# First layer of a hybrid encoder trunk: where the scalar columns, the gate's low-rank product and the squares of the second half stand in the order of work

## Chip, core and metric

One core of a Trainium2 chip runs the whole program. The metric is the device time of one execution in microseconds; the time shown is a median over several runs. The engines are called as the profile does: PE (matrix products), PEld (loading of their stationary operand), DVE (VectorE), ACT (ScalarE), POOL (GpSimd), SP (SyncE, which here issues the loads).

## What is computed

The reference is a two-layer encoder on a sequence of 1024 tokens with 1024 channels, all in float32. The first layer (even) feeds two groups of heads from one input projection of the normalised input; the second (odd) is attention over chunks. Each has a squared-ReLU MLP and a gated embedding behind it. The change touches the first layer only, of which this matters:

```python
h = rmsnorm(x, norm_mix_g[i])
proj = h @ even_w_in[e]
dh = token_shift(h) - h
# group A, RWKV-7
xw = h + dh * mu_lora[0]
xa = h + dh * mu_lora[1]
xg = h + dh * mu_lora[2]
w_log = -jax.nn.softplus(-(w0 + jnp.tanh(xw @ w1) @ w2).astype(jnp.float32)) - 0.5
a = jax.nn.sigmoid(a0 + (xa @ a1) @ a2)
g = jax.nn.sigmoid(xg @ g1) @ g2
...
y = y.reshape(bsz, seq, A_WIDTH) * g.astype(jnp.float32)
# group B, gated DeltaNet
beta = jax.nn.sigmoid(beta_logit.astype(jnp.float32))
g = -jnp.exp(a_log.astype(jnp.float32)) * jax.nn.softplus((alpha_logit + dt_bias).astype(jnp.float32))
...
gc = jnp.cumsum(g, -1)
```

`g` of group A is the gate; its low-rank products are `xg @ g1` and then `@ g2`. `beta_logit` and `alpha_logit` are eight columns of `proj`, the scalar columns; `gc` is their cumulated decay. `rmsnorm` needs the sum of squares of each token over all channels.

## The kernel before

The first layer works on the transposed input, 128 channels on the partitions and tokens along the free axis. The sequence is cut in two halves of 512 tokens (`HB`), and the heads in 4 pairs of group A ("rwkv") and 4 heads of group B ("gdn"). That makes 16 units, in the order half, pair, group (`units`, line 533): units 0, 2, 4, 6 are rwkv and 1, 3, 5, 7 gdn of the first half, 8 to 15 the same of the second.

Six lanes, written as generators, are woven together by `run` (line 135), which keeps a clock of its own and takes the first lane that is due: post, back, mid and front of a unit, the cumulated decays (`gdn_cums`), and last `l0_in`, which projects the inputs of every unit. `l0_in` is so the filler: its products are written down where no other lane is due. The tile framework then puts the instructions of each engine in an order of its own, by priority and by an estimate of when each can run, so an instruction that depends on nothing can stand far ahead of its place in the program.

`l0_in` (line 560) does this for each half. At its first unit (0 or 8) it loads the eight channel blocks of `x`, scales them into pairs of a rounded and a remainder part (`xg`), and forms the low-rank product of decay and learning rate (`lora(0, ...)`, result `lwa`). It projects the unit's inputs (`rwkv_in`, three matrices; `gdn_in`, four with the gate), each a dense product of 24 matmuls (`project`, `dense_part`). At line 644, behind the inputs of units 0 and 8, follow the scalar columns (`gdn_scalars`, line 716: 16 matmuls with the tile `wba`, an eviction to `ba`, four transposes, then some thirty operations on 16 columns, most on DVE, to `gs_beta` and `gs_g`) and the gate's low-rank product (`lora(1, ...)`, result `lgo`). Later units' inputs wait for buffers of units before them: unit u's input j needs `("raw", u - 2, j)`, and a gdn unit's gate `("front", u - 2)`.

What waits for the two: `gdn_cums` for `("g", hf)`, and then each gdn unit's front for `("gc", hf)` (line 1063); each rwkv unit's post for `("lg", hf)` (line 1050).

`lora` (line 691) loads one matrix (`lraw`), makes two scaled copies of it on POOL (line 704), and splits each into a rounded part (`whi`, ACT, line 298) and a remainder (`wlo`, DVE, line 299) before its two dense products. Loaded weights, `lraw`, its scaled copies, the raw columns of `wba`, `ba` and the second product's result `sb` are all tiles of one ring, `wraw`, of two buffers; `whi` and `wlo` have two each.

Squares for the normalisation: for the first half they are taken of the tiles just loaded. For the second half, line 632 loads `x` once more, four times two blocks through the ring `pl` of the pool `pre`, behind unit 6's inputs; `square` (line 666) squares on ACT and adds on POOL into `acc`. Unit 7 turns that into row statistics (line 641), used from unit 8 on. Unit 8 loads the second half's `x` again for `xg`, one pair through `pl` and three through `wraw` (line 574).

Of the kernel before, what the change touches and what calls it, by code (L numbers as in the profile page):

```python
# [8 lines left out]
F32 = mybir.dt.float32  # L9
# [8 lines left out]
P = 128  # L18
# [3 lines left out]
HB = 512  # L22
# [93 lines left out]
class Trunk:  # L116
# [443 lines left out]
    def l0_in(self, units):  # L560
        nc, a, fr = self.nc, self.a, self.fr
        self.state = {}
        self.xg = []
        for u, (nm, p, hf) in enumerate(units):
            if u % 8 == 0:


                self.xg, squares = [], []
                if hf == 0:
                    acc = fr.tile([P, HB], F32, tag="rsbc", name="acc", bufs=2)  # L570
                    self.w_first = self.load_w(a["w_in"][4])
                else:

                    x2 = [self.load_x(q, self.pre if q == 1 else self.wp, "pl" if q == 1 else "wraw")
                          for q in range(4)]
                for k in range(NK):
                    if hf == 0:
                        xr = self.t2()
                        nc.sync.dma_start(out=xr, in_=a["x"][k, :, 0:HB])
                    else:  # L580
                        xr = x2[k // 2][:, k % 2, :]
                    if k % 2 == 0:
                        xg2 = self.pair(k // 2)
                    xg = xg2[:, k % 2]
                    self.split_scaled(xg, xr, self.vec("mixg", k), slice(0, HB))
                    self.xg.append(xg)
                    if hf == 0:
                        squares.append(lambda k=k, xr=xr: self.square(acc, xr, k == 0))
                for f in squares:
                    f()  # L590
                if hf == 0:
                    raw = self.pre.tile([P, 2, 512], F32, tag="ph", name="wa2r")
                    for j in range(2):
                        for r in range(2):
                            nc.sync.dma_start(out=raw[64 * r:64 * r + 64, j], in_=a["wa2"][64 * j:64 * j + 64])
                    hi = self.pre.tile([P, 2, 512], F32R, tag="pl", name="wa2h")
                    nc.scalar.copy(hi, raw)
                    nc.vector.tensor_tensor(raw.bitcast(F32R), raw, hi.bitcast(F32), op=ALU.subtract)
                    self.wa2 = self.dr.tile([P, 2, 2, 512], F32, tag="wa2", name="wa2")
                    nc.sync.dma_start(out=self.wa2[:, 0], in_=hi.bitcast(F32))  # L600
                    nc.sync.dma_start(out=self.wa2[:, 1], in_=raw)
                    self.g2 = self.l0.tile([P, 512], F32, tag="g2", name="g2")
                    nc.sync.dma_start(out=self.g2, in_=a["g2"])
                    self.hv = self.l0.tile([P, 2, 4], F32, tag="hv", name="hv")
                    nc.sync.dma_start(out=self.hv.rearrange("p a b -> p (a b)"),
                                      in_=a["gdnhv"].rearrange("(o c) -> o c", o=1).broadcast_to((P, 8)))
                    self.ea = self.l0.tile([P, 1, 4], F32, tag="ea", name="ea")
                    nc.scalar.activation(self.ea, self.hv[:, 0:1, :], AF.Exp)
                sc = {}
                if hf == 0:  # L610
                    rsc = self.rsc = self.sm.tile([P, 4], F32, tag="rsc", name="rsc")
                    self.rs = fr.tile([P, HB], F32, tag="rsbc", name="rsbc", bufs=2)

                    self.extra = [lambda t=t: self.psm.tile([P, HB], F32, tag=t, name="dps") for t in ("y", "ch", "pm")]
                    self.late, self.plan = [], {2: lambda: self.row_stats([acc], rsc), 3: lambda: self.to_rows(rsc, self.rs)}
                    raws = yield from getattr(self, nm + "_in")(p, hf, u)
                else:
                    self.rs = acc
                self.pst = None
                sc["lwa"] = yield from self.lora(0, [(0, 64, 0), (64, 128, 1)], "la")  # L620
                lwa = sc["lwa"]
                nc.scalar.activation(lwa[0:64], lwa[0:64], AF.Tanh)
                sc["lwa"] = self.pre.tile([P, 2, HB], F32R, tag="ph", name="lwa")
                for j, (r, o) in enumerate(((slice(0, 64), slice(64, 128)), (slice(64, 128), slice(0, 64)))):
                    m = sc["lwa"][:, j]
                    nc.scalar.copy(m[r], lwa[r])
                    nc.vector.tensor_tensor(m[o], lwa[r], m[r].bitcast(F32), op=ALU.subtract)
            if u:
                raws = yield from getattr(self, nm + "_in")(p, hf, u)
            self.state[u] = (raws, sc)  # L630
            self.mark(("in", u), 1.0)
            if u == 6:

                acc = fr.tile([P, HB], F32, tag="rsbc", name="acc", bufs=2)
                for q in range(4):
                    x2 = self.load_x(q, self.pre, "pl")
                    for e in range(2):
                        self.square(acc, x2[:, e], q + e == 0)
            if u == 7:
                rsc = self.rsc = self.sm.tile([P, 4], F32, tag="rsc", name="rsc")  # L640
                self.row_stats([acc], rsc)
                yield "l0_in1"
                self.to_rows(rsc, acc)
            if u % 8 == 0:

                yield from self.gdn_scalars(hf, sc)
                gg = yield from self.lora(1, [(0, 128, 2)], "lg")
                nc.scalar.activation(gg, gg, AF.Tanh, scale=0.5)
                nc.vector.tensor_scalar(gg, gg, 0.5, 0.5, op0=ALU.mult, op1=ALU.add)
                sc["lg"] = gg  # L650
                self.mark(("lg", hf))

        rsb = lambda: fr.tile([P, HB], F32, tag="rsbc", name="xs", bufs=2)
        pt = [self.pair(k) for k in range(2)]
        sc = [self.pair(q, F32) for q in (2, 3)]
        sc = [t[:, e] for t in sc for e in range(2)]
        yield from self.ple_proj(0, lambda k, hf: pt[k][:, hf], sc[0], lambda n: sc[1 + n % 3], rsb, self.load_w)
        yield from self.out_early(0, a["x"], self.pair, rsb, self.load_w, [("post", 7), ("post", 13), ("post", 14), ("post", 15)])

    def load_x(self, q, pool, tag):  # L660

        x2 = pool.tile([P, 2, HB], F32, tag=tag, name="xr")
        self.nc.sync.dma_start(out=x2, in_=self.a["x"][2 * q:2 * q + 2, :, HB:T].rearrange("k p t -> p k t"))
        return x2

    def square(self, acc, x, first):

        nc = self.nc
        sq = acc if first else x
        nc.scalar.activation(sq, x, AF.Square)  # L670
        if not first:
            nc.gpsimd.tensor_tensor(acc, acc, sq, op=ALU.add)
# [123 lines left out]
    def rwkv_in(self, p, hf, u):  # L796
        raws = []
        for j in (1, 0, 2):
            if u >= 2:
                yield ("raw", u - 2, j)  # L800
            w = self.load_w(self.a["w_in"][4 * j + p]) if u or j != 1 else self.w_first
            raws.append((yield from self.project(w, f"r{p}{j}", 1)))
        return [raws[1], raws[0], raws[2]]

    def gdn_in(self, n, hf, u):
        raws = []
        for j in (1, 0, 2):
            if u >= 2:
                yield ("raw", u - 2, j)
            raws.append((yield from self.project(self.load_w(self.a["w_in"][12 + 4 * j + n]), f"g{n}{j}", 3)))  # L810
        if u >= 2:
            yield ("front", u - 2)
        gate = yield from self.project(self.load_w(self.a["w_in"][24 + n]), None, 0, "gate")
        return [raws[1], raws[0], raws[2], gate]
# [414 lines left out]
    def tail(self, i, xsrc):  # L1229
# [13 lines left out]
        with ExitStack() as es:  # L1243
# [153 lines left out]
            def end(*keys):  # L1397
                for key in keys:
                    split_end(*begun.pop(key))
            load_x(0)  # L1400
            load_x(1)
            wn = {2: self.w_next} if i == 0 else {}

# [820 lines left out]
```

## Time and profile before

| | us |
|---|---|
| median of 3 runs | 3088.87 |
| lowest and highest | 3086.13, 3096.15 |
| the profiled execution | 3095.25 |
| its span, first to last instruction | 3093.5 |

In the profiled execution DVE is busy for 72% of the span, ACT for 46% and POOL for 41%; the mean granted clock of PE is 0.969 of full speed. The first layer's sixteen units take about the first quarter of the span. Tables by stage give, for a stretch of the span, its length, then busy time and number of instructions of PE, PEld, DVE, ACT and POOL, the granted clock of PE, the share of time in which the DMA engines worked and what they moved in GB/s. Lines of a timeline give start and duration in us, engine, line of the kernel, operation, output and inputs, shapes and count; in brackets stands how long the engine was idle before and what ended that. Groups of instructions give minimum, median and maximum in ns and the first and last start in us. `SPq` is the queue of SyncE.

### The profile page before, as it was taken

To read this page: it belongs to the slowest core of one execution; us is meant where nothing else is said; L and a number is where in the kernel's file an instruction comes from. 1 tells how busy PE (TensorE), PEld (TensorE's weight loads), DVE (VectorE), ACT (ScalarE), POOL (GpSimd) and SP (SyncE) were. 2 spreads that over 40 slices of the span, in tenths; PEclk is the share of its full clock that TensorE was granted. 3 is DMA by queue.
4 is the path that set the end of the run, shared out by engine and by line. 5 is a ranking of instruction groups with operands and counts; after the bars stand their busy time and mean duration, and the time that the engine had idled before them with its cause. 6 is when DMAs were issued, how large, how long until landed. Compare 5 with 4: busy or idle time off the path is not lost. (4 is left out here: it accounts for less than half of the span.)

```text
span 3093.5 us, 45263 instructions
## 1 busy us (share of the span) xinstructions
PE 2970.1 (96%) x16888; PEld 2493.6 (81%) x16888; DVE 2220.7 (72%) x3680; ACT 1411.6 (46%) x2546; POOL 1256.6 (41%) x1396
## 2 busy tenths in 40 slices
PE   7999899999998999999999899999999999999999
PEld 5787778888786888788888899989887888788887
DVE  6556665666847888877686587877867888877672
ACT  4344443444435444443343465655645444543331
POOL 6244343433613666646354200000113666645442
PEclk8999898999898999999999999999999999999999
DMA  4222112222445333564423211110275433654322
GB/s 134 97 72 65 47 44 76 69 76 78 147 155 197 123 147 149 205 246 164 137 87 124 81 44 37 41 57 20 72 263 208 149 147 147 220 215 173 127 96 102
DMA packets 166765, 374.31 MB, mean 121 GB/s; under 512 B 41360, under 2 KB 45584, under 8 KB 165136
## 3 DMA queue, kind: packets, MB, share of 16 engines
q1 hardware_dynamic: 134288, 312.68, 29.4%
q10 hardware_dynamic: 32256, 58.73, 5.0%
q8 instruction: 133, 2.18, 0.3%
q14 instruction: 88, 0.72, 0.1%
HBM read 259.15 MB, written 112.20 MB: 120 GB/s over the span
## 5 line engine op out<-in xcount | busy, mean ns | idle before, releaser
L173 PE MATMUL dps<-r,act 128*128 128x512 f32 x4440 | 1044.0, 394 | 10.8 <-DVE act L113 9.0
L173 PEld LDWEIGHTS dps<-r,act 128*128 128x128 f32 x4440 | 835.4, 189 | 202.9 <-DVE act L113 17.0
L173 PE MATMUL dps<-xg,whi 128*128 128x512 f32 x1248 | 427.6, 419 | 22.3 <-ACT xg L342 6.7
L113 ACT CAST act<-late 128x512 fp32r<-128x512 f32 (+1 forms) x282 | 205.5, 731 | 443.6 <-DVE late L113 261.2
L113 DVE TENSOR_TENSOR act<-late,act 128x512 fp32r<-128x512 f32 (+1 forms) x282 | 331.8, 1178 | 72.2 <-ACT act L113 68.9
L173 PE MATMUL dps<-wq,act 128*128 128x384 f32 x1536 | 304.5, 346 | 7.2 <-DVE vs L1982 2.5
L173 PEld LDWEIGHTS dps<-xg,whi 128*128 128x128 f32 x1248 | 240.4, 198 | 73.7 <-ACT xg L342 6.7
L173 PEld LDWEIGHTS dps<-wq,act 128*128 128x128 f32 x1536 | 266.1, 191 | 12.2 <-DVE vs L1982 4.1
L173 PE MATMUL dps<-xg,wlo 128*128 128x512 f32 x624 | 257.8, 414 | 1.5 <-DVE wlo L299 1.5
L113 POOL TENSOR_TENSOR late<-late 128x512 f32<-128x512 f32 (+1 forms) x104 | 189.6, 1832 | 76.3 <-ACT late L113 57.9
L113 POOL TENSOR_TENSOR late<-late,rs 128x512 f32<-128x512 f32 x88 | 136.7, 1566 | 103.3 <-DVE late L113 95.3
L1989 POOL TENSOR_TENSOR sq<-qk 128x512 f32<-128x512 f32 x32 | 35.8, 1117 | 315.3 <-ACT qk L1977 289.7
L113 DVE TENSOR_TENSOR r<-act,r 128x1024 fp32r<-128x1024 f32 (+1 forms) x80 | 141.4, 1770 | 6.7 <-ACT r L113 6.7
L173 PEld LDWEIGHTS dps<-xg,wlo 128*128 128x128 f32 x624 | 122.4, 196 | 27.4 <-DVE wlo L299 2.2
L113 DVE TENSOR_TENSOR late<-late 128x512 f32<-128x512 f32 x120 | 142.3, 1186 | 1.0
L173 PE MATMUL dps<-xw,act 128*128 128x512 f32 x576 | 139.2, 394 | 3.7 <-ACT act L113 3.7
L173 PEld LDWEIGHTS dps<-xw,act 128*128 128x128 f32 x576 | 108.7, 189 | 28.5 <-ACT act L113 4.2
L2077 ACT ACTIVATE pb<-pb,mx 128x640 f32<-128x640 f32 (+4 forms) x128 | 89.5, 699 | 86.7 <-DVE mx L2075 83.7
L298 ACT CAST whi<-wraw 128x1024 fp32r<-128x1024 f32 x76 | 79.5, 1047 | 95.4 <-PE dps L173 66.5
L113 DVE TENSOR_TENSOR late<-late,dps 128x512 f32<-128x512 f32 x154 | 104.7, 682 | 19.7 <-ACT late L113 16.6
L299 DVE TENSOR_TENSOR wlo<-wraw,whi 128x1024 fp32r<-128x1024 f32 x76 | 97.1, 1278 | 28.0 <-ACT whi L298 27.8
L113 ACT ACTIVATE late<-late 128x512 f32<-128x512 f32 x176 | 110.6, 630 | 13.5 <-POOL late L113 9.8
(504 smaller groups left out, 5829.8 us busy)
## 6 DMA issues: line engine op xcount, KB each, us to landing
late<-in_w SPq DMA_DIRECT2D x100, 512.0 KB
hc<-late ACTq DMA_DIRECT2D x154, 256.0 KB
act<-hc SPq DMA_DIRECT2D x76, 512.0 KB
wraw<-in_w_in SPq DMA_DIRECT2D x56, 512.0 KB
hraw<-hc SPq DMA_DIRECT2D x36, 512.0 KB
hc<-sums ACTq DMA_DIRECT2D x70, 256.0 KB
act<-in_w SPq DMA_DIRECT2D x28, 512.0 KB
wraw<-in_w_out SPq DMA_DIRECT2D x21, 512.0 KB
```

Source lines behind the costliest of these rows:

```text
L113: return lambda *args, **kw: self.tc.keep_in_program_order(f(*args, **kw))
L173: r = self.nc.tensor.matmul(out, lhsT, rhs, start=start, stop=stop)
L298: nc.scalar.copy(hi, raw)
L299: nc.vector.tensor_tensor(lo, raw, hi.bitcast(F32), op=ALU.subtract)
L1989: G.tensor_tensor(sq, q4[:, 8 * e:8 * e + 8], q4[:, 8 * e:8 * e + 8], op=ALU.mult)
L2077: A.activation(S, S, AF.Exp, bias=mx[:, 1:2], accum_out=l)
```

## The change

Three edits. The scalar columns and the gate's low-rank product move from behind the inputs of units 0 and 8 to behind those of units 1 and 9 (`u % 8 == 1`). The loads of the second half's `x` for the squares move from the ring `pl` to the weights' ring `wraw`. And they are written in four places, one pair of blocks behind each of unit 6's three inputs and one behind unit 7's input j = 1, not all four behind unit 6; the sum is kept as `acc2`. The operations are the same ones.

```diff
                 else:
-                    self.rs = acc
+                    self.rs = self.acc2
...
             self.mark(("in", u), 1.0)
-            if u == 6:
-
-                acc = fr.tile([P, HB], F32, tag="rsbc", name="acc", bufs=2)
-                for q in range(4):
-                    x2 = self.load_x(q, self.pre, "pl")
-                    for e in range(2):
-                        self.square(acc, x2[:, e], q + e == 0)
             if u == 7:
                 rsc = self.rsc = self.sm.tile([P, 4], F32, tag="rsc", name="rsc")
-                self.row_stats([acc], rsc)
+                self.row_stats([self.acc2], rsc)
                 yield "l0_in1"
-                self.to_rows(rsc, acc)
-            if u % 8 == 0:
+                self.to_rows(rsc, self.acc2)
+            if u % 8 == 1:
 
                 yield from self.gdn_scalars(hf, sc)
                 gg = yield from self.lora(1, [(0, 128, 2)], "lg")
...
+    def early_squares(self, q):
+
+        if q == 0:
+            self.acc2 = self.fr.tile([P, HB], F32, tag="rsbc", name="acc", bufs=2)
+        x2 = self.load_x(q, self.wp, "wraw")
+        for e in range(2):
+            self.square(self.acc2, x2[:, e], q + e == 0)
...
             raws.append((yield from self.project(w, f"r{p}{j}", 1)))
+            if u == 6:
+                self.early_squares(len(raws) - 1)
...
             raws.append((yield from self.project(self.load_w(self.a["w_in"][12 + 4 * j + n]), f"g{n}{j}", 3)))
+            if u == 7 and j == 1:
+                self.early_squares(3)
```

## Prediction

> **What bounds the kernel now.** I read the page first, the table of time by stage next, then the timeline of TensorE in the stage that the change touches, and last the timelines of SyncE's DMA queue, VectorE and GpSimd for what TensorE waits for there. From the page:
>
> ```profile
> PE 2970.1 (96%) x16888; PEld 2493.6 (81%) x16888; DVE 2220.7 (72%) x3680; ACT 1411.6 (46%) x2546; POOL 1256.6 (41%) x1396
> ...
> PE   7999899999998999999999899999999999999999
> ```
>
> TensorE (PE) is busy for 96% of the span, so the change can win no more than gaps of PE, and stretches where its clock is below full. In the second line (40 slices of 77 us, busy tenths) the first slice is the emptiest, with 7; single ones with 8 follow. The table of time by stage is split where the changed code works:
>
> ```profile
> 48.00:56.00 8.00, 2.74 (x8) 1.21 (x8) 7.16 (x14) 4.15 (x9) 4.36 (x3) 0.66 0.44 149
> 56.00:68.00 12.00, 9.74 (x32) 7.21 (x32) 11.84 (x27) 5.77 (x10) 7.00 (x7) 0.66 0.16 45
> 68.00:80.00 12.00, 6.00 (x20) 4.47 (x20) 9.58 (x20) 5.25 (x10) 4.46 (x4) 0.63 0.27 89
> 80.00:90.00 10.00, 10.00 (x40) 8.02 (x39) 1.53 (x5) 2.27 (x8) 0.00 (x0) 0.77 0.19 64
> ...
> 100.00:250.00 150.00, 150.00 (x1191) 123.06 (x1189) 91.17 (x189) 59.29 (x121) 58.35 (x138) 1.00 0.24 78
> 250.00:330.00 80.00, 73.15 (x673) 61.20 (x673) 45.47 (x97) 35.45 (x83) 35.17 (x86) 0.96 0.21 62
> 330.00:350.00 20.00, 16.59 (x149) 14.15 (x149) 19.81 (x64) 10.25 (x18) 6.97 (x9) 0.77 0.08 27
> 350.00:500.00 150.00, 139.18 (x1050) 115.37 (x1049) 94.27 (x243) 59.90 (x141) 75.73 (x169) 0.85 0.18 56
> ```
>
> The columns are the stretch, its length, busy time of PE, weight loads, DVE, ACT and POOL, the clock, and DMA. From 48 to 80 us PE lacks 5.26 + 2.26 + 6.00 = 13.5 us, and it works at about two thirds of its clock; from 100 to 250 us it is full at full clock. So what is late in the first 80 us is not caught up: it is pushed through whatever follows. The timeline of PE names the gaps (in brackets the idle time before, and what ended it):
>
> ```profile
> 43.63 3.87 PE L173 MATMUL dps<-xg,wba 128*40 128x512 f32 x16
> 48.28 0.44 PE L178 MATMUL dps<-ident,ba 40*128 40x40 f32 x4 [0.78 <-DVE ba L730]
> 50.41 1.08 PE L173 MATMUL tp<-lwa,wa 128*128 128x512 f32 x2 [1.68 <-issue]
> ...
> 56.40 1.22 PE L173 MATMUL dps<-xg,whi 128*128 128x512 f32 x2 [2.91 <-ACT whi L298]
> ...
> 73.83 0.79 PE L173 MATMUL pm<-AR,pad 128*128 128x128 f32 x2 [4.38 <-ACT pad L944]
> ```
>
> This is the scalar columns of the first half (`wba`, 43.63), then their transposes (`ba`), then the gate's low-rank product (56.40), whose weights must be loaded, scaled on GpSimd and split on ACT and DVE before PE can start. The serial stretch from the end of the `wba` products (47.5) to the gate's first product (56.4) is 8.9 us long, and unit 1's inputs, 22 us of independent products, stand behind it.
>
> **The change part by part.** *First half: unit 1's inputs go ahead of scalars and gate.* Nothing is added or removed; 16 products of `wba`, two dense products of the gate and four of unit 1 change places. Ceiling of the gain: the 13.5 us of gaps, and of the clock 2.74 x 0.34 + 9.74 x 0.34 + 6.00 x 0.37 + 10.00 x 0.23 = 8.8 us, 22.3 us together. From the timelines of SyncE's queue and ACT:
>
> ```profile
> 36.31 0.34 SPq L719 DMA_DIRECT2D wraw<-in_wba  x1
> ...
> 47.54 0.34 SPq L696 DMA_DIRECT2D lraw<-in_lora  x1
> ...
> 70.70 0.34 SPq L292 DMA_DIRECT2D wraw<-in_w_in  x1
> ...
> 92.84 0.33 SPq L292 DMA_DIRECT2D wraw<-in_w_in  x1
> ...
> 96.18 1.05 ACT L298 CAST whi<-wraw 128x1024 fp32r<-128x1024 f32 x1 [3.79 <-DMA wraw<-in_w_in]
> ```
>
> The ring `wraw` has two buffers. One came free at 36.31 and one at 47.54; now the first two matrices of unit 1 take them, and the queue is in order, so the later loads follow. A load takes 96.18 - 92.84 = 3.3 us, a split 1.05 us on ACT before PE can begin. The first matrix is there by 41 us, ahead of 43.6, where PE has finished the decay's low-rank product; a dense product lasts some 5.5 us at full clock (24 matmuls of 0.23 us, the spacing in the timeline). The second, if it gets the buffer of 47.54, is ready at 47.5 + 3.3 + 1.05 = 51.9, against 49.1 when the first product ends: a gap of 2.8 us that the products on `lwa` (1.08 us and as much again) partly fill. I leave 2 us of it. From there unit 1 flows until about 68 us.
>
> The 8.9 us chain of scalars and gate now follows unit 1. Its cover is unit 0's work, the 6.00 us that PE did between 68 and 80. I leave 8.9 - 6.0 = 2.9 us as idle, and since short gaps here went with a clock of 0.66, another 5 us of slow products. Gain: 22.3 - 2 - 2.9 - 5 = **12 us**. Both ends: 0, if unit 0's work isn't there in time to cover the chain, and 22.
>
> [...]
>
> What waits for the moved work has room:
>
> ```profile
> L788 DVE COPY gs_gc<-dps x1: 175/175/175, 80.8 to 80.8; 128x16 f32<-128x16 f32 x1
> ...
> L178 PE MATMUL tp<-ident,gs_gc x4: 271/272/272, 107.7 to 113.5; 128*128 128x128 f32 x4
> ```
> ```profile
> L788 DVE COPY gs_gc<-dps x1: 174/174/174, 477.2 to 477.2; 128x16 f32<-128x16 f32 x1
> ...
> L178 PE MATMUL tp<-ident,gs_gc x8: 271/272/273, 525.4 to 607.5; 128*128 128x128 f32 x8
> ```
> ```profile
> L173 PE MATMUL pp<-lgo,g x16: 590/592/697, 246.2 to 930.1; 128*128 128x512 f32 x16
> ...
> L713 POOL TENSOR_TENSOR lgo<-lgo,sb x2: 1270/1278/1287, 90.4 to 490.0; 128x512 f32<-128x512 f32 x2
> ```
>
> The cumulated decays are there at 80.8 and 477.2 and first used by a unit after the change's point at 107.7 and 525.4, 27 and 48 us later; the gate of the first half is used 155 us after it is made. Moving their making behind unit 1's 22 us of products costs the waiters nothing.
>
> *Second half: the same move, around unit 9.* Unit 9's inputs wait for buffers of unit 7, the scalars do not, so a filler is exchanged for work that may be held back. VectorE, PE and GpSimd at the worst place of that stage:
>
> ```profile
> 460.33 2.96 DVE L762 TENSOR_SCALAR gs_poly<-gs_poly 128x16 f32<-128x16 f32 x1
> ...
> 466.02 0.33 DVE L1185 SCALAR_TENSOR_TENSOR Sg<-Sg,gs_egl,ch 128x128 f32<-128x128 f32 x1
> ```
> ```profile
> L762 DVE TENSOR_SCALAR gs_poly<-gs_poly x14: 157/173/2961, 62.4 to 469.7; 128x16 f32<-128x16 f32 x14
> ```
> ```profile
> 460.53 1.25 POOL L880 TENSOR_TENSOR f<-f 128x512 f32<-128x512 f32 x1
> ```
> ```profile
> 466.40 1.11 PE L173 MATMUL ch<-Vp,PMQ 128*128 128x64 f32 x4 [5.04 <-DVE Sg L1185]
> ```
>
> A 16-column step of the scalars' polynomial, 0.17 us in the median of its group, took 2.96 us while a GpSimd product of 512 columns ran; the state update `Sg` came behind it on VectorE, and PE stood for 5.04 us. The polynomial moves; this stall goes, or another chain step falls behind it. Ends: -11 us (the 5.04 and as much again of slow clock behind it) and +11 us (the same stall once more, where the filler is missing). I take 0.
>
> *Squares.* Eight ACT squares and seven GpSimd adds leave the first 72 us and go to units 6 and 7:
>
> ```profile
> L672 POOL TENSOR_TENSOR acc<-acc,xr x7: 1276/1291/2339, 37.5 to 69.5; 128x512 f32<-128x512 f32 x7
> ```
> ```profile
> L670 ACT ACTIVATE xr<-xr x7: 612/630/632, 23.8 to 60.1; 128x512 f32<-128x512 f32 x7
> ```
> ```profile
> 293.95 0.40 SPq L663 DMA_DIRECT2D xr<-in_x  x1
> ...
> 324.08 0.37 SPq L663 DMA_DIRECT2D xr<-in_x  x1
> ```
>
> That is 7 x 1.29 = 9.0 us of GpSimd and 8 x 0.63 = 5.0 us of ACT, beside engines that in 250 to 330 us are busy 35.17 and 35.45 of 80. The program puts them at unit 6 already, but their ring `pl` was free, so they ran at once; the three loads of this kind that go through `wraw` (unit 8's; the first and the last are shown) were held in line until 293.95, so the new ones will be too. The cost is the ring: an x pair holds a buffer for a load (3.3), two squares (1.2) and two adds (2.6), some 7 us, four times, while the queue behind it waits. Cover is the interval of weights there, from the rows of the splits on VectorE:
>
> ```profile
> 247.25 1.22 DVE L299 TENSOR_TENSOR wlo<-wraw,whi 128x1024 fp32r<-128x1024 f32 x1
> ...
> 302.45 1.25 DVE L299 TENSOR_TENSOR wlo<-wraw,whi 128x1024 fp32r<-128x1024 f32 x1 [1.25 <-ACT whi L298]
> ```
>
> five splits in 55.2 us, one per 13.8. So 7 us fit. I take a cost of 2 us for a pair that meets a busy GpSimd; ends 0 and 24 (below). The sums of squares are needed by statistics only after unit 7's inputs, so they are no wait by themselves.
>
> **Sum:** -12 + 0 + 2 = -10 us. The profiled execution took 3095.25 us (span 3093.5), 6.4 over the median 3088.87; a difference carries over, so 3088.9 - 10 = **3079 us**.
>
> **The rivals.** *A, the forecast:* half the ceiling comes back at the start, the rest cancels: 3079, with 3073 to 3086 around it.
> *B, all of it:* PE flows from 43 us and the stall at 466 goes too: -22 - 5 + 2 = -25, 3064. For: the VectorE rows above; against: the 8.9 us chain still exists, and nothing says that a queue reordered by its priorities puts unit 0's work just there.
> *C, absorbed:* the recurrences of the heads bind from 250 us on, and PE only waits there for as long as it was early: 3089. For: 250 to 500 us is the stage with gaps and a clock of 0.77 to 0.96. Against: 100 to 250 us has no gap at all, so the chains run no later than PE lets them.
> *D, slower, the weights' ring:* GpSimd works in order and is held by the triangular inverses.
>
> ```profile
> 253.10 0.49 POOL L407 TENSOR_SCALAR_AFFINE_SELECT sub<-subb 32x256 f32<-32x256 f32 x1 [6.56 <-DMA subb<-scr]
> ...
> 269.96 1.11 POOL L417 COPY sub<-sub 32x256 f32<-32x256 f32 x1
> ```
>
> One inverse takes 253.10 to 271.07, 18 us. An x pair that meets one holds its buffer for 7 + 18 = 25 us, and SyncE's queue waits with it. It decides from 13.8 us of holding on; two of four pairs hit cost 2 x 11 = 22 us, with the 12 won at the start 3088.9 - 12 + 22 = 3099. Against: in those 18 us other work of GpSimd was let in between the steps, so the adds may be too.
> [...]
> *E, the change doesn't do what it says:* the x loads are hoisted as before and take the ring at the start; the rows at 293.95 to 324.08 speak against it, and its time is near 3089.
>
> **How the numbers follow.** A 0.45, B 0.15, C and E 0.22, D 0.18. A change of 0.3%, 9.3 us, is about what a measurement of this kernel can tell from none. A lies on that line: 0.28 of its 0.45 beyond it, 0.17 inside. Faster 0.28 + 0.15 = 0.43; same 0.17 + 0.22 = 0.39; slower 0.18. The range takes in A, C and the nearer parts of B and D: 3063 to 3098.
>
> **What would show it.** The end of unit 1's inputs in VectorE's timeline:
>
> ```profile
> 113.26 0.69 DVE L685 TENSOR_TENSOR gate<-dps,rsbc 128x512 f32<-128x512 f32 x1 [3.64 <-PE dps L173]
> ```
>
> Right: in 43 to 68 us PE has no gap over 3 us and its clock is near 1; the gate projection of unit 1 is evicted near 70 us instead of at 113.26; the squares run between 240 and 330 us; 100 to 250 us stays full. Wrong: a gap of over 6 us behind the `wba` products; waits of PE for `whi` or of SyncE for x pairs of over 10 us at 240 to 340 us (D); the gain of the first 100 us no longer there at 500 us (C).

## The result and the profile after

| | before | after |
|---|---|---|
| median, us | 3091.73 | 3064.19 |
| lowest and highest, us | 3086.13, 3096.15 | 3061.70, 3069.92 |
| the profiled execution, us | 3095.25 | 3063.73 |
| its span, us | 3093.5 | 3062.0 |
| mean granted clock of PE | 0.969 | 0.975 |

The ratio is 0.9908, with an interval of 0.9893 to 0.9924: the changed kernel is 28 us faster, four runs each. That lies in the range, at its lower end; the forecast of 10 us was short by almost two thirds. The page of the changed kernel, engines and slices:

```profile
PE 2958.2 (97%) x16888; PEld 2488.1 (81%) x16888; DVE 2217.9 (72%) x3680; ACT 1409.4 (46%) x2546; POOL 1255.6 (41%) x1396
...
PE   8999999998989999999999999999999999999999
```

The instructions are as many as before, on every engine. PE is busy for 2958.2 us, 11.9 less, in a span that is 31.5 us shorter: 31.5 - 11.9 = 19.6 us of its idle time went, and the rest is products at a higher clock (a mean of 0.975 where it was 0.969). The first slice has 8 instead of 7. The table by stage of the changed kernel (stretch, length, busy time and count of PE, PEld, DVE, ACT and POOL, clock, DMA):

```profile
48.00:56.00 8.00, 8.00 (x37) 6.57 (x36) 4.33 (x7) 2.72 (x4) 0.19 (x1) 1.00 0.38 136
56.00:68.00 12.00, 12.00 (x59) 9.93 (x58) 11.29 (x20) 5.21 (x10) 6.60 (x8) 1.00 0.21 67
68.00:80.00 12.00, 10.44 (x62) 7.13 (x61) 8.54 (x22) 6.09 (x16) 2.48 (x2) 1.00 0.11 44
80.00:90.00 10.00, 9.93 (x55) 8.46 (x54) 8.05 (x24) 2.81 (x5) 6.56 (x15) 1.00 0.23 61
...
100.00:250.00 150.00, 148.15 (x1209) 121.37 (x1208) 101.27 (x206) 65.88 (x137) 75.47 (x147) 0.97 0.29 93
250.00:330.00 80.00, 77.96 (x742) 64.99 (x741) 55.74 (x147) 41.80 (x95) 30.20 (x77) 1.00 0.21 60
330.00:350.00 20.00, 15.93 (x66) 13.65 (x65) 15.23 (x31) 8.60 (x22) 13.71 (x27) 0.70 0.24 84
350.00:500.00 150.00, 147.38 (x1242) 122.59 (x1244) 92.39 (x223) 59.05 (x127) 61.24 (x141) 0.93 0.20 62
```

From 48 to 90 us PE is idle for 1.6 us in place of 13.5, and its clock is 1.00 in all four rows. That is the whole ceiling of the start but for one gap. The timeline of PE shows the gap:

```profile
67.95 3.87 PE L173 MATMUL dps<-xg,wba 128*40 128x512 f32 x16
71.75 1.16 PE L173 MATMUL tp<-AR,b 64*128 64x128 f32 x8
...
77.71 0.73 PE L173 MATMUL tp<-bh,blkr 128*128 128x512 f32 x2 [1.56 <-ACT N L904]
78.28 0.60 PE L178 MATMUL pm<-ident,b 128*128 128x128 f32 x4
78.75 0.74 PE L173 MATMUL dps<-xg,whi 128*128 128x512 f32 x2
```

Unit 1's products run without a break up to the scalar columns at 67.95. From their end at 71.8 to the gate's first product at 78.75 the chain of loading, scaling and splitting is still 6.9 us long, but unit 0's small products (`tp`, `pm`) now lie in it, and only 1.56 us are left open. What ends them is unit 0's own tile `N`, not the gate's weights. SyncE's queue in the changed kernel:

```profile
35.55 13.20 SPq L292 DMA_DIRECT2D wraw<-in_w_in  x4
53.78 0.33 SPq L720 DMA_DIRECT2D wraw<-in_wba  x1
...
63.39 0.33 SPq L697 DMA_DIRECT2D lraw<-in_lora  x1
```

All four matrices of unit 1 are issued between 35.55 and 48.75, and the columns and the gate's matrix follow. VectorE's timeline has the row named as the test, 43.7 us ahead of 113.26:

```profile
69.58 0.64 DVE L686 TENSOR_TENSOR gate<-dps,rsbc 128x512 f32<-128x512 f32 x1
```

To follow what becomes of this I use one measure for all kernels, the **lead**: the table by stage in rows of 25 us, busy time of PE times granted clock, summed from the start, minus the same sum of the kernel before. It tells how many us of full-clock products a kernel is ahead. The changed kernel's lead is 21 us at 100 us, 21 at 225, 15 at 250, 22 at 300, 23 at 325, 39 at 500, 18 at 775, 25 at 1000 and 30 at 3000. So the start gives 21, another 16 come between 325 and 500 us, about as much goes again between 600 and 775, and the gain is made by 1000 us, in the first layer. The measure is rough: before_row_pool below, whose time doesn't differ, has a lead of 5 at 1000 us, and after_front4 has 32 at 3000 us with a span that is 22 us shorter.

### The profile page after: what moved, and what is told of

Same layout as the page of the kernel before. It is cut to its first block, busy times and chain, and to the rows that moved or that the text cites. A ratio compares the mean times of both kernels' runs of the same rounds, so it can differ in the third digit from the quotient of the medians.

```text
span 3062.0 us, 45242 instructions
## 1 busy us (share of the span) xinstructions
PE 2958.2 (97%) x16888; PEld 2488.1 (81%) x16888; DVE 2217.9 (72%) x3680; ACT 1409.4 (46%) x2546; POOL 1255.6 (41%) x1396
## 5 line engine op out<-in xcount | busy, mean ns | idle before, releaser
L173 PEld LDWEIGHTS dps<-r,act 128*128 128x128 f32 x4440 | 836.2, 189 | 199.9 <-DVE act L113 16.1
L173 PE MATMUL dps<-xg,whi 128*128 128x512 f32 x1248 | 421.4, 416 | 14.6 <-ACT xg L342 7.1
```

The source lines that it names most:

```text
L173: r = self.nc.tensor.matmul(out, lhsT, rhs, start=start, stop=stop)
```

## The experiments

The table gives all runs in the order of the text. The us are (1 - ratio) times the time before; the ratio is taken from all runs of both kernels, and the difference of the two medians is up to 3 us off it. The shift of unit 1's gate (113.26 before), that of the last product on the second half's gate (`pp<-lgo`, at 930 us before) and that of the span are from the profiled executions. The one of before, 3095.25 us, lies 3.5 us above its median of four, so the shifts of the span come out some us too large.

| kernel | ratio | interval | us | lead at 100, 325, 500, 1000 us | unit 1's gate | last use of gate | span |
|---|---|---|---|---|---|---|---|
| the change | 0.9908 | 0.9893-0.9924 | -28 | 21, 23, 39, 25 | -43.7 | -25.7 | -31.5 |
| first_only | 0.9855 | 0.9840-0.9870 | -45 | 20, 23, 53, 56 | -41.4 | -50.6 | -42.8 |
| second_only | 0.9982 | 0.9971-0.9993 | -6 | 0, -1, 4, 5 | -0.9 | -8.3 | -8.4 |
| both_moves | 0.9876 | 0.9859-0.9892 | -38 | 19, 19, 42, 49 | -41.0 | -43.9 | -43.3 |
| squares_only | 0.9954 | 0.9939-0.9970 | -14 | 5, -3, 17, 19 | -4.8 | -16.1 | -20.1 |
| gate_only | 0.9968 | 0.9956-0.9980 | -10 | 4, 2, 17, 11 | -16.7 | -14.9 | -13.9 |
| scalars_only | 0.9945 | 0.9930-0.9959 | -17 | 11, 6, 28, 17 | -18.7 | -17.1 | -21.3 |
| before_nudged | 0.9991 | 0.9981-1.0001 | -3 | -2, -2, -5, -2 | +1.2 | 0.0 | -2.3 |
| first_nudged | 0.9904 | 0.9887-0.9920 | -30 | 20, 18, 49, 35 | -41.3 | -33.5 | -32.8 |
| before_front4 | 1.0020 | 1.0010-1.0029 | +6 | -1, -2, -3, -8 | +1.4 | +10.1 | +9.0 |
| first_front4 | 0.9927 | 0.9901-0.9954 | -23 | 21, 15, 33, 25 | -42.0 | -22.9 | -25.8 |
| after_front4 | 0.9928 | 0.9902-0.9954 | -22 | 20, 19, 41, 31 | -42.3 | -26.3 | -21.9 |
| gate_at_2 | 0.9945 | 0.9926-0.9964 | -17 | 23, 11, 26, 18 | -41.8 | -16.2 | -18.4 |
| before_row_pool | 1.0003 | 0.9991-1.0014 | +1 | 0, 1, 1, 5 | +0.2 | -1.0 | -6.2 |
| both_front4 | 0.9896 | 0.9881-0.9912 | -32 | 19, 14, 34, 33 | -40.7 | -31.3 | -33.9 |
| after_nudged | 0.9925 | 0.9908-0.9942 | -23 | 20, 19, 34, 23 | -44.4 | -23.5 | -25.0 |

### The change in its parts

Four kernels ran together, each with a part of the change. The theory was that the move of the first half gives the time; the rivals, that the squares' departure from the start does, or the second half's move.

*The first half alone.* The squares stay in `pl`, behind unit 6.

```diff
+            if u == 6:
+
+                self.acc2 = fr.tile([P, HB], F32, tag="rsbc", name="acc", bufs=2)
+                for q in range(4):
+                    x2 = self.load_x(q, self.pre, "pl")
+                    for e in range(2):
+                        self.square(self.acc2, x2[:, e], q + e == 0)
...
-            if u % 8 == 1:
+            if u in (1, 8):
...
-            if u == 6:
-                self.early_squares(len(raws) - 1)
...
-            if u == 7 and j == 1:
-                self.early_squares(3)
```

> Only the first half's scalars and gate product go behind unit 1's inputs; second half and squares as before. Theory 1 (the start): the gaps and the low clock of 48 to 90 us go, the work done by 100 us is some 22 us ahead as in the changed kernel, and PE pushes it through: 18 to 24 us below the kernel before. Theory 2 (the squares): while the squares stay in the first 72 us, ACT, GpSimd and SyncE's queue keep holding up unit 1's weights: 4 to 10 us below. Theory 3 (the second half): most of the 28 us come from 250 to 500 us, so 0 to 8 us below.

Measured: 3050.72 beside 3093.88 us, 45 us faster, 17 more than the whole change. Tables by stage of first_only and of the kernel before:

```profile
43.00:100.00 57.00, 54.41 (x261) 43.10 (x260) 41.38 (x81) 27.34 (x51) 32.85 (x53) 0.97 0.33 99
325.00:500.00 175.00, 169.08 (x1371) 138.51 (x1373) 124.32 (x302) 79.02 (x180) 81.63 (x182) 0.99 0.22 66
```
```profile
43.00:100.00 57.00, 42.99 (x166) 31.38 (x165) 36.81 (x70) 20.94 (x40) 23.28 (x24) 0.76 0.29 91
325.00:500.00 175.00, 160.77 (x1234) 133.74 (x1233) 117.57 (x313) 75.15 (x175) 85.22 (x183) 0.84 0.18 54
```

At the start 54.41 x 0.97 - 42.99 x 0.76 = 20 us are won, with the squares where they were: the first half's move does this. From 325 to 500 us, 169.08 x 0.99 - 160.77 x 0.84 = 32 us more are won, though first_only leaves the work of that stage as it is. Of these 32, 8 us are idle time that goes; the other 24 are clock, 160.77 us of products at 0.99 where it was 0.84. The theory named the right edit, and its 18 to 24 us are about half of what the edit did.

*The second half alone.* Squares as in first_only.

```diff
-            if u % 8 == 1:
+            if u in (0, 9):
```

> Only the second half's scalars and gate product go behind unit 9's inputs. Theories 1 and 2: within 5 us of the kernel before, the start as before. Theory 3: 12 to 25 us below, with the 5 us wait of PE for the state update at 466 us gone and the clock from 350 to 500 us above 0.85.

Measured: 3086.91 beside 3093.88, 0.9982 (0.9971 to 0.9993): 6 us faster. The lead appears between 325 and 500 us and is 3 to 7 us from there on. The wait of 5.04 us at 466 is gone here: PE's longest wait for `Sg` from 325 to 500 us is 1.4 us. So that wait isn't worth the 12 to 25 us of the third theory, and this part isn't the source of the gain.

*Both moves, squares as before.*

```diff
-            if u % 8 == 1:
+            if u in (1, 9):
```

> Both moves, squares as before (written behind unit 6, loaded through the ring pl, so run in the first 72 us). Theories 1 and 3: 22 to 30 us below, so nearly all of the change's 28. Theory 2: no more than 15 us below, and gaps of PE of several us between 43 and 68 us.

Measured: 3053.78, 0.9876 (0.9859 to 0.9892), 38 us faster, 10 more than the change with the squares, whose interval begins at 0.9893. The gain is there without the squares' move, so that rival falls as the source.

*The squares alone*, through `wraw` as in the change:

```diff
-            if u % 8 == 1:
+            if u in (0, 8):
```

> Only the squares move to units 6 and 7 through the weights' ring; scalars and gate as before. Theory 1: the chain from the scalars' products to the gate's weights stays 8.9 us long, so within 5 us of before. Theory 2: 12 us or more below, with the gaps at 50 to 60 us shorter by half or more. If the ring holds up the weights (rival D of the prediction): 5 us or more above.

Measured: 3079.51, 0.9954 (0.9939 to 0.9970), 14 us faster. Neither side's mechanism shows: only 5 us of lead are there at 100 us, they are gone at 325, and 20 come from 325 to 500.

### Is the gain behind 325 us a property of the order, or luck?

Part of the gain comes in stages that the edits don't touch. To see if it hangs on the order of instructions at large, I changed one number of the table of latencies by which `run` and the lanes plan, in kernels with and without the move. This changes no work, only what is written down next to what.

```diff
-    "l0_in1": 1.35,
+    "l0_in1": 5.00,
```

> The kernel before with one number of its planning table changed: the latency l0_in1, used once, at unit 7's row statistics, from 1.35 to 5.00. No work, tile or dependency changes; only the order in which the lanes are woven from unit 7 on. Theory L (order by chance): what the kernels win or lose from 325 to 750 us beyond the lead of the start depends on how the lanes happen to fall; the time moves by 5 to 25 us, and the lead at 300 us stays 0. Theory S (structure): the loss of 39 us from 330 to 500 us in the kernel before comes from being late at unit 8 and needs the earlier start to go; the time stays within 4 us.

> The kernel with only the first half's move, and the same number of the planning table changed. Theory L: the lead at 300 us stays 22, and the time moves by 5 to 25 us, more likely up, as 45 us below the kernel before is the best seen. Theory S: within 4 us of the unnudged kernel, and the gain from 325 to 500 us stays some 30 us.

Measured: before_nudged 3090.31 beside 3092.91, -3 us with an interval up to 1.0001; first_nudged 3061.29, -30 us. Tables by stage of before_nudged and of first_nudged:

```profile
325.00:500.00 175.00, 159.65 (x1252) 133.45 (x1251) 117.93 (x313) 75.68 (x176) 84.03 (x181) 0.83 0.17 53
```
```profile
325.00:500.00 175.00, 169.24 (x1450) 140.18 (x1450) 124.67 (x305) 80.58 (x184) 84.72 (x186) 0.99 0.22 68
```

With this nudge, the start (lead 20) and the gain from 325 to 500 us (31) stand as in first_only. What falls is later: the lead goes from 49 at 500 to 35 at 1000, where first_only keeps 53 and 56. So 15 of the 45 us hang on a number that has nothing to do with the move. Neither theory came out whole: first_only moved by 15 us, as L has it, and the kernel before by 3, as S has it.

A second number, with the same four questions:

```diff
-    "gdn_front1": 6.00,
+    "gdn_front1": 4.00,
```

> The kernel before with the planning table's latency gdn_front1 at 4.00 instead of 6.00: every gdn unit's front is woven in 2 us earlier, from unit 1 on (after the first 100 us, and ahead of the stage from 325 us). No work, tile or dependency changes. Theory L (order by chance in the stage of units 5 to 9): the 39 us that the kernel before loses from 330 to 500 us shrink by 8 us or more, and the time falls by 5 to 30 us with no lead at 100 us. Theory S (an early start is needed): the loss in that stage stays within 5 us, and so does the time.

> The kernel with only the first half's move, with the same 4.00. The lead at 100 us stays 20 under both theories. Theory L: the gain of 30 us from 325 to 500 us changes by 8 us or more, the time with it. Theory S: within 5 us of the kernel with only the first half's move.

> The changed kernel with the same 4.00. The lead at 100 us stays 21. Theory L: time 3045 to 3085, more than 5 us from the changed kernel's 28 us below. Theory S: within 5 us of it.

Measured: before_front4 3099.41 beside 3093.69, +6 us (L had it 5 to 30 us faster, S within 5); first_front4 3069.25, -23; after_front4 3070.55, -22. The tables by stage of before_front4 and first_front4:

```profile
325.00:500.00 175.00, 161.73 (x1278) 133.57 (x1277) 115.69 (x314) 74.27 (x174) 84.89 (x180) 0.83 0.16 49
```
```profile
325.00:500.00 175.00, 169.41 (x1310) 138.56 (x1309) 115.73 (x280) 71.50 (x161) 83.24 (x178) 0.91 0.21 64
```

The kernel before loses what it did in this stage under either nudge (160.77, 159.65 and 161.73 us busy at 0.83 to 0.84). first_front4 wins 18 us there, not 30, and gives 9 back by 1000 us. Its lead at 100 us is 21. So the start is robust, and what follows is not: first_only is 45, 30 or 23 us ahead of the kernel before with three settings of two numbers. Each beside the kernel before with the same setting, the move is worth 45, 27 and 29 us.

*The change under the first nudge:*

> The changed kernel with l0_in1 at 5.00. The lead at 300 us stays 22 us. If its gain from 325 to 500 us and the loss behind it are the order's, the time is anywhere from 15 to 45 us below before; if they belong to the structure, 28 us below within 5.

Measured: 3071.15 beside 3090.92, 0.9925 (0.9908 to 0.9942). The three versions of the change, 28, 22 (front4) and 23 us (this one), have intervals that overlap; I don't tell them apart.

### Which of the two moved parts frees the start?

The first move takes two things out of unit 1's way. Each was left in its place alone, for the first half; the second half and the squares stay as before.

*The gate's product moved, the scalars left:*

```diff
-            if u % 8 == 1:
-
+            if u in (0, 8):
                 yield from self.gdn_scalars(hf, sc)
+            if u in (1, 8):
                 gg = yield from self.lora(1, [(0, 128, 2)], "lg")
```

> First half: only the gate's low-rank product goes behind unit 1's inputs, the scalar columns stay behind unit 0's; second half and squares as before. Theory A (the gate's weights): the gap at the start is the wait for the gate's scaled weights, with unit 1's loads queued behind them in the ring of two buffers; so nearly all of the lead comes back: 17 to 22 us of full-clock work ahead at 100 us. Theory B (the scalars): it is the scalars' tile ba in the ring and their thirty small operations on DVE that hold up unit 0 and the weights: less than 10 us ahead at 100 us. The whole time is the lead at 100 us and whatever the second half does, so -10 to -45 us under A and -10 to +5 under B, by theory L below.

*The scalars moved, the gate's product left:* the same edit with the two conditions exchanged.

> First half: only the scalar columns go behind unit 1's inputs, the gate's product stays behind unit 0's. Theory A: 0 to 6 us ahead at 100 us, as the wait for the gate's weights stays. Theory B: 12 us or more ahead at 100 us.

Measured: gate_only 3082.82 beside 3092.91, 10 us faster; scalars_only 3073.79, 17 us faster. The leads at 100 us are 4 and 11 (6 from 125 us on); together the two parts give 20. Neither part alone has the gain, and they don't add up: A asked for 17 to 22 us of lead in gate_only, B for 12 or more in scalars_only, and neither came. SyncE's queue and PE in gate_only:

```profile
35.60 0.33 SPq L728 DMA_DIRECT2D wraw<-in_wba  x1
...
48.25 1.40 SPq L292 DMA_DIRECT2D wraw<-in_w_in  x2
```
```profile
48.84 0.44 PE L178 MATMUL dps<-ident,ba 40*128 40x40 f32 x4 [0.78 <-DVE ba L739]
51.12 1.19 PE L173 MATMUL tp<-lwa,wa 128*128 128x512 f32 x2 [1.84 <-issue]
54.05 1.22 PE L173 MATMUL dps<-xg,whi 128*128 128x512 f32 x2 [1.74 <-ACT whi L298]
...
70.35 0.80 PE L173 MATMUL py<-Sh,AR 128*128 128x128 f32 x2 [7.63 <-POOL AR L913]
```

The same two views of scalars_only:

```profile
36.19 0.34 SPq L705 DMA_DIRECT2D lraw<-in_lora  x1
...
60.05 0.34 SPq L292 DMA_DIRECT2D wraw<-in_w_in  x1
```
```profile
50.40 1.19 PE L173 MATMUL tp<-lwa,wa 128*128 128x512 f32 x2 [7.09 <-issue]
```

Read the queue first. The buffer that comes free at 36 us goes to whichever of the two is ahead, `wba` or `lraw`, and unit 1's first matrix is issued at 48.25 or at 60.05, where the change issues it at 35.55. PE then lacks unit 1's products: gaps of 0.78, 1.84 and 1.74 us behind the `wba` products in the one, 7.09 us from 43.3 on in the other. In gate_only PE waits 7.63 us more for unit 0's tile `AR`. In that stretch VectorE does the scalars' 16-column steps between the steps of unit 0's chain, and two of them, 0.17 us in the median, take 1.2:

```profile
64.25 1.23 DVE L771 TENSOR_SCALAR gs_poly<-gs_poly 128x16 f32<-128x16 f32 x1
65.52 1.20 DVE L770 TENSOR_TENSOR gs_poly<-gs_poly,gs_s 128x16 f32<-128x16 f32 x1
```

`AR` is done there at 70.3 us, where the change has it at 66.3, and the remainder `wlo` of unit 1's third matrix comes on VectorE at 68.05 only. That the two long steps delay these is read from the order on VectorE, and not tried by itself. Against the change, gate_only lacks 7 us of full-clock products from 43 to 62.7 us and 10 us from 62.7 to 80. So in scalars_only the loss follows the ring directly; in gate_only the larger part lies behind the wait for `AR`. What frees the start is that both leave; how much of it is the ring alone isn't shown, since no run gave the ring a third buffer.

*The gate one unit later still*, scalars behind unit 1:

```diff
-            if u % 8 == 1:
-
+            if u in (1, 8):
                 yield from self.gdn_scalars(hf, sc)
+            if u in (2, 8):
                 gg = yield from self.lora(1, [(0, 128, 2)], "lg")
```

> First half only: scalars behind unit 1's inputs, the gate's low-rank product behind unit 2's; second half and squares as before. The chain from the scalars to the gate's weights, which left one gap of 1.6 us in the changed kernel, then has unit 2's products beside it: the lead at 100 us is 20 to 22 again, no more than 2 us better. The gate of the first half is first used at 220 us or later, so no new wait there. Under S the time is that of the kernel with only the first half's move (45 us below before) within 5 us; under L anywhere from 20 to 50 us below.

Measured: 3076.99 beside 3093.69, 17 us faster. Its table by stage:

```profile
43.00:100.00 57.00, 55.70 (x275) 44.31 (x274) 41.60 (x83) 26.99 (x51) 30.05 (x48) 1.00 0.34 108
```

PE is busy for 55.70 of 57 us at full clock, and the lead at 100 us is 23, 20 from 125 us on: there is nothing more to win at the start. The time lies outside what either theory gave (S: 45 us below before, within 5; L: 20 to 50 below). The kernel ends 28 us behind first_only, from which it differs in this edit alone: its lead is 11 by 325 us where first_only has 23, and it wins 15 from there to 500 where first_only wins 31. Why isn't known.

### A collision at 325 to 500 us, and the price of the squares

The kernel before loses in that stage what the others don't. One theory was that unit 7's row statistics stand on VectorE in the way of the heads' recurrences there. The option `pool=True` makes them on GpSimd.

```diff
-                self.row_stats([acc], rsc)
+                self.row_stats([acc], rsc, pool=True)
```

> The kernel before, with the thirteen small operations of unit 7's row statistics (the inverse root) on GpSimd instead of VectorE. Theory C (a collision on VectorE): the stage from 330 to 500 us loses 39 us because three chains of small operations stand together on VectorE at 338 to 348 us, ahead of the state update and of the next unit's matrix; without one of them that stage does at least 8 us better and the time is 8 to 20 us below. If not C: the stage stays within 5 us, the time within 6.

Measured: 3092.80 beside 3090.92, 1.0003 (0.9991 to 1.0014). Table by stage:

```profile
325.00:500.00 175.00, 159.66 (x1225) 131.81 (x1223) 116.90 (x302) 74.39 (x172) 87.27 (x197) 0.85 0.17 53
```

Nothing moves; that theory falls. This run and before_front4 also settle what the wait of 5.04 us at 466 is worth. The longest waits of PE from 445 to 480 us, in before_front4 and then in before_row_pool:

```profile
466.39 0.80 PE L173 MATMUL ch<-U,b 128*128 128x128 f32 x2 [2.09 <-ACT U L1179]
```
```profile
465.59 2.04 PE L173 MATMUL tp<-AR,b 64*128 64x128 f32 x8 [3.29 <-DVE b L886]
```

The long wait is gone in both, and neither gains in the stage: other waits stand in its place.

both_moves was 10 us faster than the change, so the squares seemed to cost 10 us beside the moves. A second pair, under the second nudge (both_moves with `"gdn_front1": 4.00`):

> Both moves, squares as before, with gdn_front1 at 4.00 as in the nudged kernels. If the squares cost 10 us by themselves, it is some 10 us below the changed kernel under the same nudge (which was 0.9928 of before), so 30 to 36 us below before. If the 10 us are the order's: no fixed sign, within 12 us of that kernel either way.

Measured: 3061.51 beside 3090.92, 0.9896 (0.9881 to 0.9912), against 0.9928 (0.9902 to 0.9954) of after_front4: 10 us again, but these two intervals overlap, so this pair doesn't show it. In the first pair the largest loss lies from 600 to 800 us, in the tables by stage of both_moves and then of the changed kernel:

```profile
600.00:800.00 200.00, 188.65 (x1483) 159.26 (x1481) 147.98 (x341) 94.70 (x207) 100.52 (x185) 0.96 0.29 95
```
```profile
600.00:800.00 200.00, 186.52 (x1562) 155.91 (x1561) 139.09 (x317) 89.77 (x212) 97.01 (x184) 0.91 0.24 78
```

188.65 x 0.96 - 186.52 x 0.91 = 11 us are lost there, 370 us behind the last of the moved squares. For the nudged pair the same rows give 6, but there the kernel with the moved squares was 7 us ahead at 500 us. From 325 to 500 us the two pairs have opposite signs, and alone the squares' move gained 14 us. No run here shows a loss at the ring itself; that the squares cost 10 us in every order isn't shown, and by what link they do in the first pair stays open.

## Why the prediction was right or wrong

**The start: the right mechanism, its size too small.** This is the term that failed, 12 us where 20 came. The ceiling of 22.3 us was read well: the change leaves the 1.56 us gap, and 22.3 - 1.6 = 20.7 stands against a lead of 21. What was wrong are the three remainders that the sum took off.
- 2 us for unit 1's second matrix: none. 47.54 was taken as the time at which the second buffer comes free; it was only the time at which the old order used it. In the change all four loads are issued by 48.75, and PE has no gap.
- 2.9 us of idle in the chain to the gate: 1.56, and that for unit 0's `N`. The cover was there, as unit 0's products do fall into the chain.
- 5 us of slow products behind it: none, at a clock of 1.00. This was the largest and had the weakest ground: the 0.66 of before was taken to go with any short gap. That it came out at none has some luck in it: in first_only the clock halves at this very place, from 79.0 to 82.4 us, which costs 1.7 us.

All nine kernels with both parts of the first move have unit 1's gate 41 to 44 us earlier and a lead of 19 to 23 us at 100 us, whatever else they hold. With 21 us in place of 12 the sum would have given 19, still 8 short of the result.

The lead passes through 100 to 225 us whole. The stretch to 250 us doesn't stay full, as the prediction asked: its last 25 us have PE busy for 23.41 at a clock of 0.80, and the lead falls to 15. It is back at 22 by 300 and 39 at 500, so rival C, which has the gain absorbed, falls.

**What waits for the moved work** waits no longer, though the room is smaller than before. Rows of the changed kernel for the cumulated decays:

```profile
L178 PE MATMUL tp<-ident,gs_gc x32: 270/273/323, 92.6 to 772.1; 128*128 128x128 f32 x32
...
L789 DVE COPY gs_gc<-dps x2: 165/170/176, 88.3 to 469.3; 128x16 f32<-128x16 f32 x2
```

They are made at 88.3 and 469.3 and first used by a unit at 92.6 and 475.3, 4 and 6 us later where it was 27 and 48; PE has no wait for them in the trace.

**The second half at 0** held within what can be told: -6 us alone, and beside the first (both_moves against first_only, with intervals that overlap) +7 by the ratios, +3 by the medians. The stall at 466 us did go, as half of the reasoning had it; the 11 us that this was to bring did not come, as second_only and the two runs above show. In the group of the changed kernel the longest step of the polynomial is 0.475 us, where it was 2.96:

```profile
L763 DVE TENSOR_SCALAR gs_poly<-gs_poly x14: 163/175/475, 82.4 to 462.9; 128x16 f32<-128x16 f32 x14
```

**The squares at +2** were wrong in place and in bounds. Groups of GpSimd and the queue of SyncE in the changed kernel:

```profile
L673 POOL TENSOR_TENSOR acc<-acc,xr x7: 1276/1283/1305, 192.8 to 232.9; 128x512 f32<-128x512 f32 x7
```
```profile
186.67 0.40 SPq L656 DMA_DIRECT2D xr<-in_x  x1
...
223.48 0.37 SPq L656 DMA_DIRECT2D xr<-in_x  x1
```

They ran at 187 to 233 us, not at 240 to 330: the weights are fetched ahead, and the x pairs stand in the queue where they are written, in the full stretch of PE. No wait of PE for them is in the trace. One sign that was named for D is there, without its cost: SyncE's queue stands for 25.9 us ahead of an x pair of unit 8 (at most 11.6 before), while PE is busy for 77.96 us of 250 to 330 at a clock of 1.00, where it was 73.15 at 0.96. So rival D falls. A gain had been left out of the bounds (0 to 24) without a reason, and alone the edit gained 14.

**What the sum did not hold at all.** 28 - 20 = 8 us are no term of it. They are what is left of 16 us won from 325 to 500 us, 18 lost from 600 to 775 and 7 won back by 1000. The price of rival B, 3064, is the measured time, and of its two reasons the first, the flow from 43 us on, is shown. Its other 5 us were to come from the stall at 466; that stall went, but where it went without the first half's move it brought nothing in before_front4 and before_row_pool, and second_only is 6 us faster (2 to 9 by the interval). So the stall's share isn't shown, and that B's price was met to the us has luck in it, as the 16, 18 and 7 us are no terms of it either.

**Open:** why the kernel before loses from 325 to 500 us, under both nudges and with the statistics elsewhere, what edits of the first 100 us recover even where they leave no lead (squares_only and gate_only are at -3 and 2 us at 325, and win 20 and 15 by 500); and why both_moves ends 10 us ahead of the change. Two versions were faster than the change clear of its interval, first_only and both_moves. Of first_only's 45 us some 20 are shown as structure; beside the kernel before with the same nudge it is at 27 and 29, so I'd not carry the number 45 anywhere.

## What to carry to other kernels

A gap in the busiest engine ahead of a long stretch where it is full was worth its whole length here, and the slow clock around it (a lead of 21 us of a ceiling of 22.3); look there for who holds the ring's buffer that the next dense work needs, and move all holders, as either half of the move left most of the start's gain behind. Ahead of crediting a small gain to an edit in a kernel whose order comes from a planner, nudge a number of the planner that changes no work, in both kernels: here that moved times by -3 to +22 us. Subtract remainders from a ceiling only with a row for each.

## What the runs showed of the hardware

In the first 100 us of these traces the granted clock has two values, 1.00 and 0.50, and a row between them is a mean over time. Rows of 0.1 us show the switches. In the kernel before the clock falls at 19.8, 50.5 and 71.0 us and rises at 23.2, 64.1 and 84.6; in the change it falls at 20.5 alone and rises at 23.9. From 43 us on it falls in gate_only at 50.8 and 64.4 and rises at 57.6 and 78.1; in scalars_only it falls at 48.1 and rises at 58.3; in first_only it falls at 79.0 and rises at 82.4. The times from one of these falls to the rise behind it are 3.4, 6.8, 10.2 and 13.6 to 13.7 us: multiples of some 3.4. The stretches of that length ahead of the last four switches of before, in a table by stage:

```profile
47.10:50.50 3.40, 0.94 (x7) 0.45 (x6) 2.22 (x5) 2.35 (x4) 0.41 (x1) 1.00 0.86 275
60.80:64.10 3.30, 3.30 (x9) 2.56 (x9) 3.30 (x7) 1.60 (x2) 2.39 (x3) 0.50 0.01 2
67.60:71.00 3.40, 0.55 (x3) 0.30 (x2) 3.38 (x6) 0.62 (x1) 3.27 (x3) 1.00 0.00 0
81.20:84.60 3.40, 3.40 (x10) 2.63 (x9) 0.18 (x1) 0.29 (x3) 0.00 (x0) 0.50 0.31 123
```

Ahead of the two falls in it PE was busy for 0.94 and 0.55 us of 3.4 (1.68 and 1.69 ahead of the early falls of before and the change, 1.10 and 1.72 in gate_only, none in scalars_only, 1.94 in first_only); ahead of both rises it was busy throughout, as it was for 3.40 us ahead of 23.2 in before and ahead of 23.9 in the change. The fall at 50.5 came behind gaps of 0.78 and 1.68 us, ahead of the one of 2.91, and the one in first_only behind gaps of no more than 0.75. In the change the lone gap of 1.56 us left the clock at 1.00, and a stretch of 3.4 us that holds it has as little as 1.84 us of products, less than the 1.94 ahead of the fall in first_only. So neither the longest gap nor the busy time of the 3.4 us ahead tells in these runs whether the clock falls, and what does isn't shown.

In scalars_only the gap of 7.09 us cost its own length and the slow products behind it. Its table by stage from the end of the gap on:

```profile
50.00:57.50 7.50, 6.64 (x14) 4.37 (x15) 5.97 (x8) 2.31 (x4) 4.77 (x4) 0.50 0.32 105
57.50:60.00 2.50, 2.50 (x10) 2.02 (x10) 2.47 (x8) 2.38 (x5) 0.11 (x1) 0.83 0.00 0
```

The clock is at 0.50 for 7.5 us in which PE is busy for 6.64, with breaks of 0.19 and 0.27 us behind the gap, and rises at 58.3, behind products without a break from 54.12 on. The share of busy time in the same row doesn't tell the clock: 6.64 of 7.5 us busy had 0.50 here, and 10.44 of 12 in the change had 1.00.
